# Smaller pieces on GpSimd and TensorE in the attention stage of a hybrid encoder block

## The chip, the cores and the metric

The kernel runs on one core of a Trainium2 chip. Its time is the time on the device in microseconds (us). One execution was taken by the hardware profiler; the others were only timed. TensorE does the matrix products, VectorE and ScalarE the elementwise work, GpSimd a few elementwise subtractions, and SyncE issues nearly all transfers (DMAs).

## The reference

One encoder block in float32 on 1024 tokens of 1024 channels, with 16 meta tokens in front:

```python
h = h + hybrid_mixer(rmsnorm(h, norm_mix), ...)      # pooling + gated linear attention, merged by gates
h = h + squared_relu_mlp(rmsnorm(h, norm_ffn), ...)  # relu(h w_ff1)^2 w_ff2
return rmsnorm(h, norm_final)[:, N_META:]

# in the mixer, z = u @ w_in is split into a, q, k, v, r, lr, ga, gb;
# the linear attention goes over chunks of 64 tokens, 4 heads (keys of 64, values of 128):
b = cumsum(a_c); decay = exp(-|b_t - b_s|)
o = (q k decay) v + (q exp(b)) S
S = exp(b_end) S + (k exp(b_end - b))^T v
m = sigmoid(ga) * y_a + sigmoid(gb) * y_b;  return m @ w_out
```

The meta tokens form a short first chunk; what the attention takes from them is the state S with which the first full chunk starts.

## The kernel before

**Split products.** Every float32 product is made of three products of rounded operands. An operand x is split into a high part (ScalarE copies it to a rounded type) and a low part (x minus the high part, by VectorE or GpSimd). `mm3` (L249 to L254) issues high x high, high x low and low x high for each of the 128-row slices, all added in one PSUM bank. Weights go through a ring of two slots: `Ring.top_up` (L76) loads a block of 1024 columns into a raw slot, splits it (L83 on ScalarE, L84 on `self.eng`) and has it ready one block ahead. `self.eng` is VectorE, but GpSimd from `gla_open` to the end of `gla`. Tiles of the raw, high and low parts are called raw, w1h and w1l.

**Stages.** From 0 to about 290 us come the norm, the gates, q, the pooling path and the first half of the values. From about 290 to 495 us runs the attention stage, `gla`; then the merge, where y_b is finished for the second half of the tokens and the product with w_out begins (about 495 to 560 us); then the feed-forward part to the end.

**The order in the attention stage.** TensorE's order is written out by hand, in the order in which the program issues. ScalarE, VectorE, GpSimd and SyncE are ordered by the framework's planner, from its own estimates of when things are ready; from `early_gates` on, the orders of ScalarE and VectorE are written out too. `gla` has two sorts of work:

- *Chains*, Python generators that issue one step and yield a number of us to be covered: `inside` (for a pair of heads and a half of the tokens: log decay, then scores and six levels of scores, L1187, each masked into the tile scc by VectorE, L1250, while VectorE and ScalarE grow the operands n and f of the next level, L1219 to L1221), `across` (transpose the keys, L1268; state updates, L1276 and then eight dependent VectorE steps, L1282; products with the values, L1289 and L1299; square, sum and norm, L1308 to L1313; transpose, L1317; multiply and split, L1318 to L1321), and `meta_state` (the meta tokens' state: a decay chain of small VectorE steps to L1157, a transposition on TensorE, L1160, its copy by VectorE, L1162, and, when the values are there, a small product, L1169).
- *Filler*: the key projections, the second value block `v_second` (9 tiles of 128 tokens, 24 products of 256 columns each, the last for the 16 meta tokens), the gates gb, and y_b for the first half of the tokens (`yb_block`; its low parts by GpSimd, L1105). Each filler chunk yields its estimated length: 0.64 us for three products of 512 columns, 2.56 us for a value tile.

In each round every live chain makes a step, and then `pour` issues filler for the largest wait asked for, times 1.1 (`PACE`), carrying what was poured too much to the next round:

```python
def pour(us):
    owed[0] += us
    while owed[0] > 0:
        cost = next(filler, None)
        if cost is None:
            return
        owed[0] -= cost
```

The chains of the second unit of the attention are `meta_state(1)`, `across` of the first unit and `inside` of the second, stepped in this order. Three PSUM banks (two of tag mm, one of tag mx) take turns for filler and meta steps.

**The merge.** `yb_block` for the second half multiplies by the gate (L1100), adds the pooling path (L1101) and splits (L1104, L1105); `load_wo` splits the blocks of w_out (L1402, L1403) that SyncE fetches (L1394). The fetch of the first blocks waits until the buffers of the attention stage, in whose place they land, have been read for the last time.

Of the kernel before, what the change touches and what calls it, by code (L numbers as in the profile page):

```python
# [8 lines left out]
F32 = mybir.dt.float32  # L9
# [3 lines left out]
ALU = mybir.AluOpType  # L13
# [6 lines left out]
KT = D // P  # L20
HALF = 512
# [37 lines left out]
class Ring:  # L59
# [16 lines left out]
    def top_up(self):  # L76
        while self.loaded < min(self.done + self.depth, len(self.queue)):
            s = self.loaded % self.depth
            if not self.fetched:
                self.fetch(1)  # L80
            raw, n = self.fetched.pop(0)
            hi, lo = self.hi[:, s, :n], self.lo[:, s, :n]
            self.nc.scalar.activation(hi, raw, ACT.Copy)  # L83
            self.eng.tensor_tensor(lo, raw, hi.bitcast(F32), ALU.subtract)  # L84
            self.views[self.loaded] = (hi, lo)
            self.loaded += 1

# [24 lines left out]
def kernel(  # L112
# [10 lines left out]
    act, dve, pool, pe = nc.scalar, nc.vector, nc.gpsimd, nc.tensor  # L123
# [20 lines left out]
    def bank(tag):  # L144
        if tag in rota:
            turn_of[tag] = turn_of.get(tag, -1) + 1
            tag = rota[tag][turn_of[tag] % len(rota[tag])]
        return psp[tag].tile([P, 512], F32, name=f"b_{tag}", tag=tag)
# [37 lines left out]
    raw = Raw(nc, [left.push(f"raw{i}", [P, D], F32) for i in range(2)])  # L186
# [10 lines left out]
    def f32(ap):  # L197
        return ap.bitcast(F32)
# [49 lines left out]
    def mm3(ps, n, lhs, rhs, first=True, last=True, more=False):  # L248

        for i in range(n):  # L250
            (ah, al), (bh, bl) = lhs(i), rhs(i)
            pe.matmul(ps, ah, bh, start=first and i == 0, stop=False, skip_group_check=more)  # L252
            pe.matmul(ps, ah, bl, start=False, stop=False, skip_group_check=more)  # L253
            pe.matmul(ps, al, bh, start=False, stop=last and i == n - 1, skip_group_check=more)  # L254
# [221 lines left out]

    vm = gB[32 : 32 + META, : 2 * 256]

    def v_tile(i, t, later=False, by_part=False):

        vw, w = S["vw"][i], 256 + 16 * (i == 0)
        if t == 8:
            half, at, n = 0, 0, META
        else:
            half, n = t // 4, P
            at = OFF[half] + (t % 4) * P
        b = bank("mm")[:n, :w]
        th, tl, hi, lo = TH[half][:, :, at : at + n], TL[half][:, :, at : at + n], vw[:, 0], vw[:, 1]
        parts = {"hh": (th, hi), "lh": (tl, hi), "hl": (th, lo)}
        left_of = {"n": 3}  # L490

        def part(name):
            left_of["n"] -= 1
            l, r = parts[name]
            for k in range(KT):
                pe.matmul(b, l[:, k], r[:, k], start=name == "hh" and k == 0, stop=left_of["n"] == 0 and k == KT - 1)

        if not by_part:
            mm3(b, KT, lambda k: (th[:, k], tl[:, k]), lambda k: (hi[:, k], lo[:, k]))

        def leave():
            if t == 8:
                act.activation(vm[:, i * 256 : i * 256 + 256], b[:, :256], ACT.Copy)
            else:
                act.activation(S["v"][i][:, t], b[:, :256], ACT.Copy)

        def leave_lr():
            if i == 0:
                act.activation(S["lrtok"][:n, t], b[:, 256:], ACT.Copy)

        if by_part:
            return part, (leave, leave_lr)
        if later:
            return leave, leave_lr
        leave()
        leave_lr()
# [87 lines left out]
    def start():  # L604
# [50 lines left out]
        with tc.manual_schedule(engines={mybir.EngineType.Activation, mybir.EngineType.DVE, mybir.EngineType.Pool}):  # L655
# [29 lines left out]
            hi(1)  # L685
            lr_lo = lr()
            v0, leave0 = v_tile(0, 0, by_part=True)
            v1, leave = v_tile(0, 1, by_part=True)
            v0("hh")
            for fn in lows[0]:  # L690
# [325 lines left out]

    def v_second():
        for t in range(9):
            v_tile(1, t)
            yield 24 * 256 / 2400  # L1020

    def yg_open():
        right.pop_to(0)
# [17 lines left out]
    def yb_load(n, h):  # L1041

        if n >= 8 or (n, h) in staged:
            return
        d = 2 * YB[h][n // 2] + n % 2
        gl, ml = staged[n, h] = (nxt("t2"), nxt("o2")) if h else (nxt("t1"), nxt("o"))
        nc.sync.dma_start(gl, gb_dram[d, h])
        nc.sync.dma_start(ml, ma_dram[d, h])
# [20 lines left out]
            yb_load(n, 1)  # L1069

    kept = {}

    def yb_block(n, h):
        j = YB[h][n]

        def fn(*wbs):
            if h == 0 and n > 1:
                kept[j] = wbs[0]
            wb = wbs[0] if wbs else kept[j]
            hi, lo = (t.rearrange("p (k c) -> p k c", k=4) for t in wb)  # L1080
            assert h or ("o", 0) in done
            yg = S["yg"][h]
            for e in range(2):
                d, w = 2 * j + e, slice(e * P, (e + 1) * P)
                for m in range(2 + h):
                    yb_load(2 * n + e + m, h)
                gl, ml = staged[2 * n + e, h]
                b = bank("mm")
                for k in range(4):
                    mm3(  # L1090
                        b, 1, lambda i: (hi[:, k, w], lo[:, k, w]),
                        lambda i: (yg[:, 0, k], yg[:, 1, k]), first=k == 0, last=k == 3,
                    )
                    yield 3 * 512 / 2400
                if e and not wbs:
                    W1.done, W1.kept = W1.done + 1, W1.kept - 1
                    W1.top_up()
                elif e:
                    yield "keep" if j in kept else "free"
                dve.tensor_tensor(gl, b, gl, ALU.mult)  # L1100
                dve.tensor_tensor(gl, gl, ml, ALU.add)  # L1101
                th = MH[h][:, d]
                tl = ML[h][:, d]
                act.activation(th, gl, ACT.Copy)  # L1104
                (dve if h else pool).tensor_tensor(tl, gl, f32(th), ALU.subtract)  # L1105

        return fn

# [5 lines left out]
    for p in range(2):  # L1114
        step(fill, k_block(p), W1, [w_cols(C_K + p * P)])
        told(("k", p))
    step(fill, v_second)
    step(fill, yg_open)
    told("v")
# [9 lines left out]
    def log_decay(lrT, p, n, dst, y, t, tag="ms"):  # L1129

        b, k = bank(tag)[:, :n], slice(0, 64 + RANK)
        pe.matmul(b, wgu[k, p * P : (p + 1) * P], lrT[k], start=True, stop=True)
        act.activation(y, b, ACT.Identity, bias=bgate[:, p : p + 1])
        act.activation(t, y, ACT.Abs)
        act.activation(t, t, ACT.Exp, scale=-1.0)
        act.activation(t, t, ACT.Ln, bias=1.0)
        dve.scalar_tensor_tensor(dst, y, 0.0, t, ALU.min, ALU.subtract)
# [4 lines left out]
    def twice(pre, suf, m):  # L1142

        pv, sv = blocks(pre, m), blocks(suf, m)
        nb = pre.shape[1] // (2 * m)
        end = lambda u: pv[:, :, u, m - 1 : m].broadcast_to([P, nb, m])
        dve.tensor_tensor(sv[:, :, 0], sv[:, :, 0], end(1), ALU.add)
        dve.tensor_tensor(pv[:, :, 1], pv[:, :, 1], end(0), ALU.add)

    def meta_state(p):  # L1150
        pre, suf, y, t = (metab[:, i] for i in range(4))
        log_decay(lrT_meta, p, META, pre, y, t, "mm")
        dve.memset(suf, 0.0)
        for m in (1, 2, 4, 8):
            twice(pre, suf, m)
        act.activation(y, suf, ACT.Exp, scale=1.0 / TAU)
        dve.tensor_tensor(y, y, S["kq"][0][:, p, 0, 0:META], ALU.mult)  # L1157
        yield 5.0
        b = bank("mm")
        pe.transpose(b[:META, :P], y, ident)  # L1160
        kt = gB[32 : 32 + META, 2 * 256 : 2 * 256 + P]
        dve.tensor_copy(kt, b[:META, :P])  # L1162
        yield 1.0
        while p and "v" not in done:
            yield 1.0
        b = bank("mm")
        for e in range(2):
            r = slice(e * CH, (e + 1) * CH)
            pe.matmul(  # L1169
                b[r, :P], kt[:, r], vm[:, (2 * p + e) * P : (2 * p + e + 1) * P], start=True, stop=True,  # L1170
                tile_position=(32, e * CH),
            )
        dve.tensor_copy(S["S"][:, 0, p], b[:, :P])
# [150 lines left out]
    def gla():  # L1324
# [12 lines left out]
        while ("k", 0) not in done:  # L1337
            next(filler)
        units = [(0, 0), (1, 0), (0, 1), (1, 1)]
        old, side = [], [meta_state(0)]  # L1340
        for n, u in enumerate(units + [None]):
            if u is None:
# [418 lines left out]
```

## Time and profile before

| | us |
|---|---|
| median of 3 runs | 1229.89 (1229.45 to 1230.79) |
| the profiled execution | 1232.42 |
| its span, first to last instruction | 1230.7 |
| TensorE busy | 1203.8 (98%) |
| VectorE busy | 856.4 (70%) |
| ScalarE busy | 618.4 (50%) |
| GpSimd busy | 54.1 (4%) |

PE is TensorE, PEld its weight loads, DVE VectorE, ACT ScalarE, POOL GpSimd, SP SyncE (SPq its queue). Rows of a timeline give the start in us from the span's start, the duration, the engine, the line, the operation and "written tile <- read tiles"; in brackets stands how long the engine was idle before and which instruction released it. In the table of waits an arrow points from the waiting instruction to the one waited for. Products overlap, so the spacing of their starts counts, not their durations.

### The profile page before, as it was taken

Reading aid. Unit: us, or ns where it says so; the run is one execution under the profiler, and the core shown is the slowest. Engines: PE = TensorE matmul, PEld = TensorE weight load, DVE = VectorE, ACT = ScalarE, POOL = GpSimd, SP = SyncE. Lnnn points to the kernel's source line nnn. Section 1 sums busy time; section 2 is a strip of 40 time slices with the busy share of each in tenths; the row PEclk is TensorE's granted clock in tenths of the full one; section 3 lists DMA queues with packets and bytes.
Section 4 is the critical chain, followed back from the end, with each engine's and each line's share of the span. In section 5 each row is a group of like instructions: output and inputs, shape, how many; then the busy total and the mean of one; then the engine's idle time right before and its main releaser. Section 6 shows DMA issues by size and latency. Waiting matters only on the chain.

```text
span 1230.7 us, 18292 instructions
## 1 busy us (share of the span) xinstructions
PE 1203.8 (98%) x6818; PEld 1002.2 (81%) x6818; DVE 856.4 (70%) x1399; ACT 618.4 (50%) x1099; POOL 54.1 (4%) x62
## 2 busy tenths in 40 slices
PE   7999999999999999999999999999999999999997
PEld 7878888978887877788878888888888888888885
DVE  7986675743566677734897676676775887887685
ACT  7677566322446753323655454554554444444544
POOL 2000000001101114000000000000000000000000
PEclk9999999999999999999999999999999999999999
DMA  8043326156102146651244444543569973333532
GB/s 252 2 113 121 117 86 189 52 171 189 36 19 72 59 154 215 209 201 52 104 134 157 145 154 148 167 155 129 177 216 329 335 251 99 99 94 95 171 95 86
DMA packets 141673, 173.85 MB, mean 141 GB/s; under 512 B 9944, under 2 KB 81392, under 8 KB 141584
## 3 DMA queue, kind: packets, MB, share of 16 engines
q1 hardware_dynamic: 141552, 172.62, 43.4%
q8 instruction: 54, 0.88, 0.3%
q14 instruction: 35, 0.29, 0.1%
q0 software_dynamic: 32, 0.07, 0.1%
HBM read 119.17 MB, written 53.48 MB: 140 GB/s over the span
## 4 chain that ended last, share of the span: by engine, by line
PE 84%; DVE 9%; ACT 3%; issue 2%; DMA 1%; POOL 0%; SPq 0%; DVEq 0%; ACTq 0%; POOLq 0%
PE b_mm L252 10%; PE b_mm L253 10%; PE b_mm L254 10%; PE b_ms L253 9%; PE b_ms L252 9%; PE b_ms L254 9%; PE b_x L253 8%; PE b_x L252 8%; PE b_x L254 8%; PE b_sc L1187 1%; PE b_mx L252 1%; PE b_m L1289 1%; DVE t L1101 1%; PE b_mx L254 1%; PE b_mx L253 1%
## 5 line engine op out<-in xcount | busy, mean ns | idle before, releaser
L252 PE MATMUL b_mm<-th,w1h 128*128 128x512 f32 (+1 forms) x312 | 118.3, 379 | 1.9 <-DVE c L800 1.0
L253 PE MATMUL b_mm<-tl,w1h 128*128 128x512 f32 (+1 forms) x312 | 116.7, 374 | 0.6 <-DVE tl L1464 0.6
L254 PE MATMUL b_mm<-th,w1l 128*128 128x512 f32 (+1 forms) x312 | 116.5, 373 | 0.0
L252 PE MATMUL b_x<-th,w1h 128*128 128x512 f32 (+1 forms) x240 | 90.8, 378 | 0.0
L253 PE MATMUL b_x<-tl,w1h 128*128 128x512 f32 (+1 forms) x240 | 90.7, 378 | 0.0
L254 PE MATMUL b_x<-th,w1l 128*128 128x512 f32 (+1 forms) x240 | 90.4, 377 | 0.0
L270 ACT ACTIVATE w1h<-raw 128x512 fp32r<-128x512 f32 x96 | 59.5, 621 | 32.8 <-PE b_ms L253 15.7
L271 DVE TENSOR_TENSOR w1l<-raw,w1h 128x512 fp32r<-128x512 f32 x96 | 65.7, 685 | 9.3 <-ACT w1h L270 9.3
L252 PEld LDWEIGHTS b_mm<-th,w1h 128*128 128x128 f32 x312 | 58.9, 189 | 13.5 <-issue 1.4
L270 ACT ACTIVATE w1h<-fs 128x512 fp32r<-128x512 f32 x72 | 45.3, 630 | 47.2 <-PE b_ms L253 32.2
L253 PEld LDWEIGHTS b_mm<-tl,w1h 128*128 128x128 f32 x312 | 59.1, 189 | 10.7 <-DVE tl L1464 0.9
L254 PEld LDWEIGHTS b_mm<-th,w1l 128*128 128x128 f32 x312 | 59.1, 189 | 10.5
L270 ACT ACTIVATE w1h<-bt 128x512 fp32r<-128x512 f32 x44 | 27.8, 632 | 67.1 <-issue 62.8
L271 DVE TENSOR_TENSOR w1l<-fs,w1h 128x512 fp32r<-128x512 f32 x72 | 49.3, 686 | 15.4 <-ACT w1h L270 15.3
L1618 DVE TENSOR_TENSOR bt<-w,w 128x512 f32<-128x512 f32 x80 | 54.8, 685 | 1.3 <-DMA w<-in_w_ff_dram 1.3
L254 PEld LDWEIGHTS b_x<-th,w1l 128*128 128x128 f32 x240 | 45.2, 188 | 8.5
L252 PEld LDWEIGHTS b_x<-th,w1h 128*128 128x128 f32 x240 | 45.1, 188 | 8.4
L253 PEld LDWEIGHTS b_x<-tl,w1h 128*128 128x128 f32 x240 | 45.1, 188 | 8.2
L270 ACT ACTIVATE fxh<-bt 128x512 fp32r<-128x512 f32 x36 | 22.8, 632 | 55.7 <-issue 50.1
L253 PE MATMUL b_ms<-wo,w1h 128*128 128x512 f32 x128 | 49.8, 389 | 0.0
L254 PE MATMUL b_ms<-wo,w1l 128*128 128x512 f32 x128 | 49.8, 389 | 0.0
L252 PE MATMUL b_ms<-wo,w1h 128*128 128x512 f32 x128 | 49.8, 389 | 0.0
(448 smaller groups left out, 3345.9 us busy)
## 6 DMA issues: line engine op xcount, KB each, us to landing
hf_dram<-h SPq DMA_DIRECT2D x112, 256.0 KB, 2.1
raw<-hf_dram SPq DMA_DIRECT2D x112, 256.0 KB, 2.7
w<-in_w_ff_dram SPq DMA_DIRECT2D x64, 256.0 KB, 4.5
raw<-in_w_in_dram SPq DMA_DIRECT2D x24, 512.0 KB, 4.7
raw<-in_w_ff_dram SPq DMA_DIRECT2D x16, 512.0 KB, 4.1
rawx<-in_w_ff_dram SPq DMA_DIRECT2D x16, 512.0 KB, 4.0
xs<-in_x_dram SPq DMA_DIRECT2D x8, 512.0 KB, 6.0
rawx<-in_w_in_dram SPq DMA_DIRECT2D x8, 512.0 KB, 4.4
```

The lines of the kernel that those rows point to most:

```text
L252: pe.matmul(ps, ah, bh, start=first and i == 0, stop=False, skip_group_check=more)
L253: pe.matmul(ps, ah, bl, start=False, stop=False, skip_group_check=more)
L254: pe.matmul(ps, al, bh, start=False, stop=last and i == n - 1, skip_group_check=more)
L270: act.activation(hi, a, ACT.Copy)
L271: dve.tensor_tensor(lo, a, f32(hi), ALU.subtract)
L1101: dve.tensor_tensor(gl, gl, ml, ALU.add)
L1187: pe.matmul(b[to, e, j], kk[r, s], qq[r, s], start=True, stop=True, tile_position=(e * CH, u * CH))
L1289: pe.matmul(o[part(u), e, j], scc[part(u), e, j], v[part(u), j, e], start=j == 0, stop=False, tile_position=(u * CH, u * CH), skip_group_c ...
L1618: dve.tensor_tensor(bt, w, S["w2"][q[3:]][:, i], ALU.add if q[2] == "+" else ALU.subtract)
```

## The change

Three edits. GpSimd's low parts are made in pieces of 256 columns: four in the ring, where GpSimd is its engine, and two in `yb_block` for the first half of the tokens; VectorE's stay whole. `v_second` issues each value tile as four quarters (two of the eight 128-row slices, six products), each yielding 0.64 us, and ScalarE's copy that empties the tile follows when the next chunk is asked for. `meta_state(1)` makes one empty step ahead of its transposition.

```diff
@@ Ring.top_up
-            self.eng.tensor_tensor(lo, raw, hi.bitcast(F32), ALU.subtract)
+            step = n if self.eng is self.nc.vector else n // 4
+            for at in range(0, n, step):
+                c = slice(at, at + step)
+                self.eng.tensor_tensor(lo[:, c], raw[:, c], hi[:, c].bitcast(F32), ALU.subtract)
@@ v_tile
-    def v_tile(i, t, later=False, by_part=False):
+    def v_tile(i, t, later=False, by_part=False, by_k=False):
...
-        if not by_part:
-            mm3(b, KT, lambda k: (th[:, k], tl[:, k]), lambda k: (hi[:, k], lo[:, k]))
+        def rows(k, n):
+            mm3(
+                b, n, lambda i: (th[:, k + i], tl[:, k + i]), lambda i: (hi[:, k + i], lo[:, k + i]),
+                first=k == 0, last=k + n == KT,
+            )
+
+        if not by_part and not by_k:
+            rows(0, KT)
...
+        if by_k:
+            return rows, leave
@@ v_second
         for t in range(9):
-            v_tile(1, t)
-            yield 24 * 256 / 2400
+            rows, leave = v_tile(1, t, by_k=True)
+            for k in range(0, KT, 2):
+                rows(k, 2)
+                yield 6 * 256 / 2400
+            leave()
@@ yb_block
+    halves_of_half = [slice(k * HALF // 2, (k + 1) * HALF // 2) for k in range(2)]
...
-                (dve if h else pool).tensor_tensor(tl, gl, f32(th), ALU.subtract)
+                if h:
+                    dve.tensor_tensor(tl, gl, f32(th), ALU.subtract)
+                for c in halves_of_half[: 2 - 2 * h]:
+                    pool.tensor_tensor(tl[:, c], gl[:, c], f32(th[:, c]), ALU.subtract)
@@ meta_state
         yield 5.0
+        if p:
+            yield 0.0
         b = bank("mm")
         pe.transpose(b[:META, :P], y, ident)
```

## The prediction

> **What bounds the kernel now.** I read the chain that ended last first, by engine, on the page; then a table of busy time by stretch; then the waits of TensorE.
>
> ```profile
> PE 84%; DVE 9%; ACT 3%; issue 2%; DMA 1%; POOL 0%; SPq 0%; DVEq 0%; ACTq 0%; POOLq 0%
> ```
>
> ```profile
> 0.00:290.00 290.00, 281.83 (x1458) 239.50 (x1459) 200.92 (x290) 169.47 (x307) 15.80 (x42) 1.00 0.42 128
> 290.00:520.00 230.00, 221.98 (x2255) 183.92 (x2254) 147.32 (x267) 112.24 (x191) 38.31 (x21) 1.00 0.34 108
> 520.00:1230.70 710.70, 699.95 (x3109) 578.77 (x3107) 508.12 (x844) 336.65 (x601) 0.00 (x0) 1.00 0.48 157
> ```
>
> The second number of a row is the stretch's length, then come the busy times of TensorE, its weight loads, VectorE, ScalarE and GpSimd, the granted clock and the DMA share. TensorE sets the time, at full clock. Everything that the diff touches runs between 290 and 520 us: there TensorE is idle for 230.00 - 221.98 = 8.0 us, and no edit removes work from it. So 8.0 us is the most that can be won, and the question is which of TensorE's waits the edits reach.
>
> ```profile
> PE b_m L1289 <- DVE S L1282: 1.6, 1, 1.6
> PE b_m L1317 <- DVE mix L1313: 1.5, 1, 1.5
> PE b_sc L1187 <- DVE scc L1250: 1.4, 2, 0.9
> PE b_mx L1160 <- DVE metab L1157: 0.8, 1, 0.8
> PE b_mm L253 <- DVE wo L1403: 0.8, 1, 0.8
> PE b_mm L252 <- ACT wo L1402: 0.5, 1, 0.5
> PE b_x L252 <- ACT w1h L83: 0.5, 1, 0.5
> PE b_x L254 <- DVE w1l L84: 0.5, 1, 0.5
> PE b_m L1289 <- DVE W L1282: 0.2, 1, 0.2
> ```
>
> These nine lines (total, times, longest, in us) make 7.8 of the 8.0 us. Most name VectorE. VectorE's and GpSimd's timelines show why it is late (start, duration, line, tiles):
>
> ```profile
> 325.96 2.53 DVE L1219 TENSOR_TENSOR n<-n,ends 128x512 f32<-128x512 f32 x1
> 394.83 2.76 DVE L1221 TENSOR_TENSOR f<-n,ends 128x512 f32<-128x512 f32 x1
> 398.27 0.35 DVE L1282 SCALAR_TENSOR_TENSOR S<-W,ends,b_m 128x128 f32<-128x128 f32 x1
> 402.51 0.68 DVE L1221 TENSOR_TENSOR f<-n,ends 128x512 f32<-128x512 f32 x1
> 428.08 2.92 DVE L1219 TENSOR_TENSOR n<-n,mix 128x512 f32<-128x512 f32 x1
> 466.07 2.26 DVE L1282 SCALAR_TENSOR_TENSOR W<-W,ends,b_m 128x128 f32<-128x128 f32 x6
> 475.20 2.90 DVE L1101 TENSOR_TENSOR t<-t,o 128x512 f32<-128x512 f32 x1
> 493.08 1.07 DVE L1101 TENSOR_TENSOR t<-t,o 128x512 f32<-128x512 f32 x1
> ```
>
> ```profile
> 325.55 2.39 POOL L84 TENSOR_TENSOR w1l<-raw,w1h 128x1024 fp32r<-128x1024 f32 x1 [11.48 <-ACT w1h L83]
> 394.64 2.41 POOL L84 TENSOR_TENSOR w1l<-raw,w1h 128x1024 fp32r<-128x1024 f32 x1 [11.32 <-ACT w1h L83]
> 427.62 2.81 POOL L84 TENSOR_TENSOR w1l<-raw,w1h 128x1024 fp32r<-128x1024 f32 x1 [13.56 <-ACT w1h L83]
> 463.57 1.29 POOL L1105 TENSOR_TENSOR tl<-t,th 128x512 fp32r<-128x512 f32 x1 [2.42 <-ACT th L1104]
> 465.57 2.40 POOL L84 TENSOR_TENSOR w1l<-raw,w1h 128x1024 fp32r<-128x1024 f32 x1 [0.71 <-ACT w1h L83]
> 474.64 2.90 POOL L84 TENSOR_TENSOR w1l<-raw,w1h 128x1024 fp32r<-128x1024 f32 x1 [1.29 <-ACT w1h L83]
> 491.86 3.45 POOL L1105 TENSOR_TENSOR tl<-t,th 128x512 fp32r<-128x512 f32 x2 [3.15 <-ACT th L1104]
> ```
>
> L1221 takes 0.68 us when GpSimd rests (402.51) and 2.76 us under a GpSimd subtraction: it ends at 397.59, one such duration after GpSimd's end at 397.05. The same at 325.96, 428.08 and 475.20. The six L1282 at 466.07, which read one operand from PSUM, run at 0.38 us each through GpSimd's 465.57 to 467.97 and wait for nothing. So a VectorE instruction with both inputs in SBUF stands still until the running GpSimd instruction ends, and the whole VectorE queue behind it. Taking 0.69 us off, the excess is 1.84 + 2.07 + 2.23 + 2.21 + 0.38 = 8.7 us, of which TensorE's waits took 0.94 + 1.6 + 0.2 + 1.5 = 4.2, about half.
>
> **The change, GpSimd's pieces.** GpSimd's two groups (count, busy us and mean ns, idle before):
>
> ```profile
> L84 POOL TENSOR_TENSOR w1l<-raw,w1h 128x1024 fp32r<-128x1024 f32 x10 | 24.9, 2490 | 129.6 <-ACT w1h L83 129.6
> L1105 POOL TENSOR_TENSOR tl<-t,th 128x512 fp32r<-128x512 f32 x8 | 12.0, 1511 | 14.9 <-ACT th L1104 14.9
> ```
>
> Undisturbed, a 1024-column subtraction costs 2.40 us, a 512-column one 1.29: 1.11 us for 512 columns, so 0.18 fixed and 0.555 per 256, 0.735 a piece. Four pieces are 2.94 us, 0.54 more than now; two halves of L1105 are 1.47, 0.18 more. There are 10 blocks and 8 tiles: 40 + 16 = 56 pieces. The added 5.4 + 1.4 us lies on GpSimd, which is busy 38.31 of 230 us. It delays w1l; the tightest case is the block of 474.64, ready at 477.54:
>
> ```profile
> 480.43 0.39 PE L254 MATMUL b_mm<-yg,w1l 128*128 128x512 f32 x1
> ```
>
> TensorE first reads it 2.9 us later, so 0.54 us, or twice that with a VectorE instruction taken between, is hidden; without that cover each block would cost what exceeds 2.9. SyncE's reload of the raw slot (L107), which waits for the last piece, moves as much; that slot is needed a block later.
>
> What VectorE gains: at 394.83 it now waits for the first piece only, to 394.64 + 0.735 = 395.37, and ends 0.69 later at 396.06 instead of 397.59: 1.53 us earlier. Behind it in the queue stand the L1282 that end in S at 398.62, for which TensorE's L1289 waits 1.6; as they ignore GpSimd, they come 1.53 earlier: **-1.5**. At 428.08 the wait on W is gone whenever the stall falls by over 0.2: **-0.2**. At 475.20, VectorE waits to 475.28 + 0.6 (the previous VectorE instruction ends at 475.28, the piece is already dispatched), ends near 476.6 instead of 478.10: 1.5 earlier. ScalarE's square, the norm and L1313 follow in a written order, so L1317 gets its operand 1.5 earlier and its wait of 1.5 shrinks to 0.1: **-1.4**.
>
> What is late next is the merge. There the last L1105 frees the buffers for a weight load:
>
> ```profile
> SPq L1394 <- POOL tl L1105: 5.1, 1, 5.1
> ```
>
> ```profile
> 500.10 1.06 ACT L1402 ACTIVATE wo<-acc 128x1024 fp32r<-128x1024 f32 x1 [1.08 <-DMA o<-ma_dram]
> ```
>
> SyncE issues it when GpSimd ends at 491.86 + 3.45 = 495.31; 4.8 us later ScalarE splits it, and behind that, in written order, stand the operands of TensorE's waits of 0.5, 0.5, 0.5 and 0.8. With four halves and VectorE in between, GpSimd ends between 0.2 later (two extra fixed parts of 0.18, less the stall that L1101 no longer passes on) and 2.3 later: four times (0.6 + 0.69) = 5.2 from 492.44, when L1101 before it ends, is 497.6. VectorE's own order is meanwhile up to 0.4 us earlier. I take **+0.5**, near the low end, because two of the four halves fall before the next VectorE instruction with two SBUF inputs is ready.
>
> **Quarter tiles.** The planner owes 1.6 x 1.1 = 1.76 us of filler after each score level, and pours while it owes more than nothing. A whole value tile counts 2.56, so after two tiles it owes -2.21, and 1.76 more leaves -0.45: level 4 follows level 3 without filler. With quarters of 0.64 the levels are 2, 3, 3, 3 and 2 quarters apart.
>
> ```profile
> 328.01 0.28 PE L254 MATMUL b_mm<-vw,tl 128*128 128x256 f32 x1
> 328.22 0.71 PE L1187 MATMUL b_sc<-n 64*64 64x64 f32 x32
> 328.86 0.39 PE L252 MATMUL b_mx<-vw,th 128*128 128x256 f32 x1
> 331.90 0.71 PE L1187 MATMUL b_sc<-n 64*64 64x64 f32 x32
> 333.56 0.71 PE L1187 MATMUL b_sc<-n 64*64 64x64 f32 x32 [0.94 <-DVE scc L1250]
> 366.18 0.71 PE L1187 MATMUL b_sc<-n 64*64 64x64 f32 x32 [0.43 <-DVE scc L1250]
> ```
>
> The pair at 331.90 and 333.56 is that place: level 4 waits 0.94 us for the copy of level 3. Three quarters, 18 matmuls at about 0.12 us, put 2.1 us between them: **-0.94**. A change from filler to scores and back costs 328.22 - 328.01 - 0.12 = 0.09 before and 0.39 - 0.28 = 0.11 after, 0.20 us. By the same account the steps that now stand back to back get filler between them at two places (levels 3 and 4; L1289 and L1299), two changes more: **+0.4**. The wait of 0.43 at 366.18 may go, since L1299 moves away from the level before it; the next two chunks are the same, so I take 0, with -0.43 as the other end. From L1169 on the account of both kernels is the same, so the order on TensorE is too. The ScalarE copy that empties a tile is now issued when the next is asked for; three banks take turns, so nothing waits.
>
> **The meta transposition.** L1160 waits 0.8 us. One round later it stands behind four transpositions, 32 scores and three quarters, some 3 us of TensorE; its VectorE copy moves with it, no DMA does, and the only reader, L1169, comes after the last value tile either way. The instruction that takes its place, L1268, transposes a tile that the previous unit finished: **-0.8**, between 0 (if VectorE, whose order the planner chooses, is as late for the scores) and -0.84.
>
> **The sum.** -1.5 - 0.2 - 1.4 + 0.5 - 0.94 + 0.4 - 0.8 = -3.94, say -4.0. The profiled execution took 1232.42 us with a span of 1230.70; the median of the runs shown, 1229.89, is 2.5 below it. So the span should be 1226.7, the execution 1228.4, the median **1225.9**.
>
> **The rivals.** First, *the merge takes it back*: GpSimd's last halves alternate with VectorE all the way and the w_out load starts 2.3 later rather than 0.5: 1225.9 + 1.8 = 1227.7. For it: 491.86 shows one alternation already (3.45 us for two of 1.29). Against: VectorE also has instructions without two SBUF inputs there.
>
> Second, *the pieces run as one*: GpSimd's queue closes the gap between them, so VectorE still waits for all four, now 0.54 longer: at 394.83, 428.08 and 475.20 TensorE loses 3 x 0.54 = 1.6 more, and the other edits bring -0.94 + 0.4 - 0.8: +0.3, 1230.2. Against it stands the pair at 491.86: the second was released at 493.1 while the first ran, and yet VectorE's L1101, issued at 493.08, ended at 494.15, before GpSimd's end at 495.31; it got in between. [...]
>
> Third, *slower*: VectorE pays a piece for each of several instructions, where it paid one long stall before. Five of GpSimd's 18 runs stalled VectorE in the rows above; if 30 of the 56 pieces did, at 0.6 us, that is 18 us of stall, half of it TensorE's: 9.0 against 4.2 now, +4.8 - 0.8 + 0.4 = +4.4 and 1234.3. It decides from about 24 pieces on (24 x 0.3 = 7.2, +3.0 - 0.4 = +2.6). At the present share 16 pieces would, most of them for part of a piece, in places where TensorE has 1 to 3 us of filler.
>
> That the change does nothing is excluded: the ring uses GpSimd throughout this stage, and other generators are live when the added empty step is taken.
>
> **How the numbers follow.** Forecast 0.55, the merge 0.20, one piece 0.09, slower 0.16. About 0.2%, 2.5 us, is what a measurement tells from no change, so faster is below 1227.4 and slower above 1232.4. Faster: 0.52 of the forecast and 0.04 of the merge, 0.56; slower: 0.14 of the third rival; same: 0.30. The forecast's own bounds are -0.43 and -0.5 (no loss in the merge), with some 1 us for the four late waits there, to 1223.5, and the merge at the top. The range runs to 1231.0, over the first two rivals, and leaves out 0.16 above and 0.03 below.
>
> **What would show it.** Right: no VectorE instruction of 512 columns above 1.4 us between 310 and 500; L1160 and the second score wait gone; L1289's and L1317's waits below 0.3; w_out split no later after the last L1105. Wrong: VectorE at 2.9 under four pieces (second rival); many at 1.2 to 1.4 with TensorE idle over 8 us (third); waits at L252 to L254 in the merge above 3.5 us in sum (first); another order on TensorE after L1169, or on VectorE before the gates, which the planner sets anew.

## The result, and the profile after

The changed kernel takes 1225.44 us (median of 5 runs, 1224.46 to 1225.56). The kernel before, run beside it, takes 1230.79 (5 runs, 1229.45 to 1233.54). The ratio is 0.9956, with an interval of 0.9946 to 0.9967: 5.3 us faster. The profiled execution took 1225.56 us with a span of 1222.7 us (before: 1232.42 and 1230.7).

Lines of the code have moved: the ring's low part L84 is now L87, GpSimd's low part of y_b is L1123 and VectorE's L1121 (both were L1105), the scores L1187 are L1207, L1289 is L1309, L1317 is L1337, and `mm3`'s three products L252 to L254 are L255 to L257.

The chain that ended last, by engine:

```profile
PE 87%; DVE 7%; ACT 2%; issue 2%; DMA 1%; POOL 0%; SPq 0%; DVEq 0%; ACTq 0%; POOLq 0%
```

The table of busy time by stretch, cut so that its first row ends at the same work as the middle row of before (the first product with w_out comes 5.13 us earlier, so 520 has become 515):

```profile
290.00:515.00 225.00, 221.94 (x2254) 183.76 (x2253) 145.15 (x267) 112.50 (x191) 47.04 (x59) 1.00 0.34 111
515.00:1222.70 707.70, 698.22 (x3108) 577.51 (x3107) 507.73 (x844) 336.84 (x601) 0.00 (x0) 1.00 0.48 158
```

TensorE's busy time in this stretch is what it was (221.94 against 221.98 us) and its idle time went from 8.0 to 225.00 - 221.94 = 3.1 us. That is a gain of 5.0 us, all of it waits. GpSimd is busy 8.7 us longer there (47.04 against 38.31) in 59 instructions instead of 21. TensorE's waits in this stretch:

```profile
PE b_mm L256 <- DVE wo L1423: 0.8, 1, 0.8
PE b_sc L1207 <- DVE scc L1270: 0.6, 1, 0.6
PE b_x L257 <- DVE w1l L87: 0.5, 1, 0.5
PE b_mm L255 <- ACT wo L1422: 0.5, 1, 0.5
PE b_mm L256 <- DVE yg L1341: 0.3, 1, 0.3
PE b_x L255 <- ACT w1h L83: 0.2, 1, 0.2
PE b_m L1309 <- DVE W L1302: 0.2, 1, 0.2
```

The two long waits for VectorE (1.6 at the state product, 1.5 at the merge of the gates) are gone, and so is that of the meta transposition (0.8). Of the two waits for the scores' copy, the one of 0.94 is gone; the other grew from 0.43 to 0.64. One small wait is new (0.3, for yg). VectorE's timeline shows how the long ones went, at the places shown of before:

```profile
393.02 1.09 DVE L1241 TENSOR_TENSOR f<-n,ends 128x512 f32<-128x512 f32 x1
...
394.79 0.35 DVE L1302 SCALAR_TENSOR_TENSOR S<-W,ends,b_m 128x128 f32<-128x128 f32 x1
...
424.60 1.21 DVE L1239 TENSOR_TENSOR n<-n,mix 128x512 f32<-128x512 f32 x1
425.74 0.96 DVE L1243 TENSOR_TENSOR ends<-mix 128x256 f32<-128x256 f32 x1
426.62 1.22 DVE L1241 TENSOR_TENSOR f<-n,mix 128x512 f32<-128x512 f32 x1
427.76 1.51 DVE L1243 TENSOR_TENSOR ends<-ends 128x128 f32<-128x128 f32 x4
```

And GpSimd's, where "x4" is a row of four pieces and the duration runs from the first's start to the last's end:

```profile
325.41 4.26 POOL L87 TENSOR_TENSOR w1l<-raw,w1h 128x256 fp32r<-128x256 f32 x4 [11.05 <-ACT w1h L83]
...
392.82 3.27 POOL L87 TENSOR_TENSOR w1l<-raw,w1h 128x256 fp32r<-128x256 f32 x4 [10.90 <-PE b_mm L257]
...
424.13 4.30 POOL L87 TENSOR_TENSOR w1l<-raw,w1h 128x256 fp32r<-128x256 f32 x4 [13.12 <-ACT w1h L83]
...
462.01 2.82 POOL L87 TENSOR_TENSOR w1l<-raw,w1h 128x256 fp32r<-128x256 f32 x4 [0.57 <-ACT w1h L83]
...
487.05 3.73 POOL L1123 TENSOR_TENSOR tl<-t,th 128x256 fp32r<-128x256 f32 x4 [3.15 <-ACT th L1119]
```

The instruction that stood 2.76 us under one whole subtraction (L1221 then) takes 1.09 us now: it starts at 393.02, ends at 394.11, and GpSimd is at work until 396.09. So VectorE gets in after the first piece and does not wait for the four. The state S follows at 394.79 and ends at 395.14, just before the product that reads it starts. The price can be seen as well: under 325.41 three VectorE instructions stall now (by 0.2, 0.5 and 0.5 us) and under 424.13 four (by 0.5 us each), where it was one before, and four pieces take 4.3 us there instead of the 2.82 at 462.01, where VectorE runs only instructions that read one operand from PSUM. Over the whole stage VectorE's stalls (each duration less the shortest of the same instruction) sum to some 6.5 us, against some 9 before. So the pieces do not do away with the stalls: they shorten the longest ones, for which TensorE waited.

The shift of TensorE's marks between the two traces shows where the time came from, step by step:

| TensorE's mark | before | after | gained in this stretch |
|---|---|---|---|
| first meta product (L1169, now L1189) | 321.26 | 321.12 | 0.14 (there from the start) |
| second meta product | 365.32 | 363.30 | 1.88: quarters and meta step |
| state product of the second unit (L1289, now L1309) | 398.76 | 395.28 | 1.46: pieces |
| the same, third unit | 437.58 | 434.01 | 0.09: pieces |
| merge of the gates, last (L1317, now L1337) | 483.70 | 478.61 | 1.52: pieces |
| first product with w_out | 511.80 | 506.67 | 0.04: the merge |
| end of the span | 1230.70 | 1222.70 | 2.87: some 1.7 not from the change, see the last section |

Up to the w_out product the gain is 5.1 us, close to the 5.3 of the medians. In the profiled execution of before, TensorE ran at half clock for 3.4 us in the feed-forward part, which none of the edits touches; this is 1.7 of the 2.9 us by which the two spans differ behind that product. The rest was not followed up; between other kernels whose clock held there, this last part differs by as much (717.61 us in `e1_pieces_only`, 716.07 in `e4_no_pieces`).

### The profile page after: what moved, and what is told of

Read it like the earlier page. It is cut to its first block, busy times and chain, and to the rows that moved or that the text cites. A ratio compares the mean times of both kernels' runs of the same rounds, so it can differ in the third digit from the quotient of the medians.

```text
span 1222.7 us, 18359 instructions
## 1 busy us (share of the span) xinstructions
PE 1202.0 (98%) x6818; PEld 1000.4 (82%) x6818; DVE 853.9 (70%) x1399; ACT 618.9 (51%) x1099; POOL 62.7 (5%) x100
## 4 chain that ended last, share of the span: by engine, by line
PE 87%; DVE 7%; ACT 2%; issue 2%; DMA 1%; POOL 0%; SPq 0%; DVEq 0%; ACTq 0%; POOLq 0%
PE b_mm L255 10%; PE b_mm L256 10%; PE b_mm L257 10%; PE b_ms L256 9%; PE b_ms L255 9%; PE b_ms L257 9%; PE b_x L256 8%; PE b_x L255 8%; PE b_x L257 8%; PE b_sc L1207 1%; PE b_mx L255 1%; PE b_mx L256 1%; PE b_mx L257 1%; PE b_m L1309 1%; DVE ut L776 1%
## 5 line engine op out<-in xcount | busy, mean ns | idle before, releaser
L255 PE MATMUL b_mm<-th,w1h 128*128 128x512 f32 (+1 forms) x312 | 117.6, 377 | 1.6 <-DVE c L811 1.0
L257 PE MATMUL b_mm<-th,w1l 128*128 128x512 f32 (+1 forms) x312 | 115.9, 371 | 0.0
L255 PE MATMUL b_x<-th,w1h 128*128 128x512 f32 (+1 forms) x240 | 90.8, 378 | 0.0
L257 PE MATMUL b_x<-th,w1l 128*128 128x512 f32 (+1 forms) x240 | 90.3, 376 | 0.0
L255 PEld LDWEIGHTS b_mm<-th,w1h 128*128 128x128 f32 x312 | 58.6, 188 | 13.2 <-issue 1.4
L257 PEld LDWEIGHTS b_mm<-th,w1l 128*128 128x128 f32 x312 | 58.6, 188 | 10.3
L257 PEld LDWEIGHTS b_x<-th,w1l 128*128 128x128 f32 x240 | 45.1, 188 | 8.5
L255 PEld LDWEIGHTS b_x<-th,w1h 128*128 128x128 f32 x240 | 45.1, 188 | 8.4
L255 PE MATMUL b_ms<-wo,w1h 128*128 128x512 f32 x128 | 49.8, 389 | 0.0
L257 PE MATMUL b_ms<-wo,w1l 128*128 128x512 f32 x128 | 49.8, 389 | 0.0
```

## The experiments

The theory was that the pieces end VectorE's stalls (about 3 us), and that the quarters and the meta step each take away a wait of their own. A first rival was that the order did it: where the planner orders an engine, other costs can give another order, and the pieces as such bring nothing. A second was that VectorE still waits for the whole run of pieces. All diffs are against the changed kernel; "before" is always the kernel before on the same chip.

**Each part alone, and two together.** Before: 1230.08 us.

`e1_pieces_only` takes the quarters and the meta step back:

```diff
-            rows, leave = v_tile(1, t, by_k=True)
-            for k in range(0, KT, 2):
-                rows(k, 2)
-                yield 6 * 256 / 2400
-            leave()
+            v_tile(1, t)
+            yield 24 * 256 / 2400
...
-        if p:
-            yield 0.0
```

> GpSimd's pieces alone; value tiles whole, transposition where it was. The orders of TensorE, VectorE and ScalarE are then those of the kernel before, instruction by instruction. Theory of the stall: VectorE waits for a piece instead of a block, so L1289's 1.63 us and L1317's 1.53 us go, the 0.23 shrinks, the waits of 0.94 and 0.84 stay: 3.0 to 3.5 us faster than before. Rival, the order: the gain comes from the new order on the engines that the other two edits bring, and pieces alone give under 1 us.

It took 1227.09 us, ratio 0.9972 (0.9962 to 0.9983): 3.0 us faster than before. TensorE's waits:

```profile
PE b_sc L1202 <- DVE scc L1265: 1.4, 2, 0.9
PE b_mx L1175 <- DVE metab L1172: 0.8, 1, 0.8
PE b_mm L256 <- DVE wo L1418: 0.8, 1, 0.8
PE b_x L257 <- DVE w1l L87: 0.5, 1, 0.5
PE b_mm L255 <- ACT wo L1417: 0.5, 1, 0.5
PE b_mm L256 <- DVE yg L1336: 0.3, 1, 0.3
PE b_m L1304 <- DVE W L1297: 0.2, 1, 0.2
```

Both long waits are gone, and the waits of the score levels (0.94 and 0.41) and of the meta transposition are as before. Apart from the cut itself, its trace has exactly the order of before on TensorE, VectorE, ScalarE and SyncE. So the gain of 3.0 us is not a matter of order.

`e2_quarters_only` has the quarters alone (low parts whole, no empty step); `e3_meta_only` has the empty step alone (low parts whole, value tiles whole); `e4_no_pieces` has both, with whole low parts:

```diff
-            step = n if self.eng is self.nc.vector else n // 4
-            for at in range(0, n, step):
-                c = slice(at, at + step)
-                self.eng.tensor_tensor(lo[:, c], raw[:, c], hi[:, c].bitcast(F32), ALU.subtract)
+            self.eng.tensor_tensor(lo, raw, hi.bitcast(F32), ALU.subtract)
...
-                if h:
-                    dve.tensor_tensor(tl, gl, f32(th), ALU.subtract)
-                for c in halves_of_half[: 2 - 2 * h]:
-                    pool.tensor_tensor(tl[:, c], gl[:, c], f32(th[:, c]), ALU.subtract)
+                (dve if h else pool).tensor_tensor(tl, gl, f32(th), ALU.subtract)
```

> Quarter tiles alone, GpSimd in whole blocks, transposition where it was. Theory of the stall: only the wait between score levels 3 and 4 goes, 0.94 us by the row and somewhat more by the spacing of the starts, against two changes between filler and chain at 0.2 each: 0.5 to 1.0 us faster; L1289's 1.6 and L1317's 1.5 stay. Rival, the order: 2 us or more, with the waits on VectorE under GpSimd's blocks shorter than 1 us.

> The transposition one step later alone. Theory of the stall: the 0.84 us wait at L1160 goes, everything else stays: 0.7 to 1.0 us faster. Rival, a wait that takes its place: VectorE is as late for the scores in the same round, and under 0.3 us is won.

> Quarter tiles and the later transposition, GpSimd in whole blocks: the changed kernel without its pieces, with the changed kernel's orders of TensorE, VectorE and ScalarE. Theory of the stall: 1.4 to 2.0 us faster than before, the changed kernel's 2.0 us at the meta product, with L1289's and L1317's waits of 1.6 and 1.5 still there, so 3.0 to 3.6 us slower than the changed kernel. Rival, the order: within 1 us of the changed kernel.

| kernel | us | ratio to before | TensorE, first scores to second meta product |
|---|---|---|---|
| before | 1230.08 | 1 | 47.65 |
| quarters alone | 1228.45 | 0.9988 (0.9979 to 0.9996) | 45.99 |
| meta step alone | 1228.96 | 0.9991 (0.9982 to 1.0) | 46.53 |
| both | 1228.57 | 0.9988 (0.9979 to 0.9997) | 45.86 |

The last column, from the traces, is sharper than the times: the quarters alone bring 1.66 us, the meta step alone 1.12, both together 1.79. They do not add. The quarters alone brought more than the 0.5 to 1.0 us that was expected of them, the meta step about what was expected. The waits of the quarters alone say why:

```profile
PE b_m L1301 <- DVE S L1294: 1.6, 1, 1.6
PE b_m L1329 <- DVE mix L1325: 1.5, 1, 1.5
PE b_mm L253 <- DVE wo L1415: 0.8, 1, 0.8
PE b_sc L1199 <- DVE scc L1262: 0.6, 1, 0.6
```

There is no wait at the meta transposition, though it was not moved. With whole tiles the planner's account poured two tiles (5.12 us) between the last decay step and the round in which the transposition stands; with quarters it pours nine (5.76 us), and VectorE is done by then. The 0.8 us was taken away by the quarters already, and the meta step, which would have taken it alone, found nothing left but 0.1 us. The two long waits stay in all three kernels; in that with both parts:

```profile
PE b_m L1303 <- DVE S L1296: 1.6, 1, 1.6
PE b_m L1331 <- DVE mix L1327: 1.5, 1, 1.5
```

This kernel has the changed kernel's order on TensorE, VectorE, ScalarE and SyncE and still has the stalls. With `e1_pieces_only` this refutes the rival of the order from both sides.

**The size of a piece, and no GpSimd.** Before: 1230.81 us. The ring's blocks in two pieces of 512 columns (`e5_ring_512`, below) and in eight of 128 (`e6_ring_128`, the same with `n // 8`); and all these low parts by VectorE (`e8_no_gpsimd`):

```diff
-            step = n if self.eng is self.nc.vector else n // 4
+            step = n if self.eng is self.nc.vector else n // 2
```

```diff
-        W1.eng = pool
+        W1.eng = dve
...
-                if h:
-                    dve.tensor_tensor(tl, gl, f32(th), ALU.subtract)
-                for c in halves_of_half[: 2 - 2 * h]:
-                    pool.tensor_tensor(tl[:, c], gl[:, c], f32(th[:, c]), ALU.subtract)
+                dve.tensor_tensor(tl, gl, f32(th), ALU.subtract)
```

> The changed kernel with ring pieces of 512 columns instead of 256; all engines' orders as in the changed kernel. Theory of the stall (VectorE waits for the running piece alone): a piece is 1.29 us rather than 0.7, so the update of f and n under it ends about 0.5 us later, L1289 and L1317 wait some 0.4 to 0.6 us each: 0.8 to 1.3 us slower than the changed kernel, 3.9 to 4.5 faster than the one before. Rival, the pieces run as one: no difference.

> Ring pieces of 128 columns. By the rows of the changed kernel a piece of 256 takes 0.705 us undisturbed and a whole block 2.40, so each cut costs 0.14 us and a piece of 128 takes 0.44: eight are 3.4 us. Theory of the stall: no wait of TensorE in the changed kernel's attention stage is left to a ring piece but 0.15 us, so within 0.3 us of the changed kernel. Rival, more pieces catch more VectorE instructions: VectorE's excess grows and 1 us or more is lost.

> The changed kernel, but VectorE makes the low parts that GpSimd made (10 of 1.23 us and 8 of 0.69, 17.8 us more on VectorE in a stretch where it is busy 143 of 222 us). Theory: the work is worth more than the stalls it brings in pieces (about 4 us of excess left), TensorE waits for VectorE at the state updates and in the last unit: 2 to 6 us slower than the changed kernel. [...]

With 512 columns the kernel takes 1226.82 us, ratio 0.9966 (0.9953 to 0.9978), 1.4 us more than the changed kernel's median. The two intervals overlap; the traces are sharper: from the first scores to the first w_out product it is 190.33 us, against 189.12 and 189.50 in two traces of the changed kernel. VectorE's and GpSimd's timelines at the second unit:

```profile
393.39 1.66 DVE L1241 TENSOR_TENSOR f<-n,ends 128x512 f32<-128x512 f32 x1
```

```profile
393.21 2.98 POOL L87 TENSOR_TENSOR w1l<-raw,w1h 128x512 fp32r<-128x512 f32 x2 [11.18 <-PE b_mm L257]
```

VectorE comes 0.18 us after the first piece has begun and takes 1.66 us: the rest of that piece (1.29 - 0.18 = 1.1) and some 0.6 of its own. For both pieces it would have needed 2.4 + 0.6. So it waits for the piece that runs and for no more; the rival of pieces that run as one is refuted here, at a second size. TensorE's wait for S comes back as 0.5 us, and that for the gates as 0.5:

```profile
PE b_m L1309 <- DVE S L1302: 0.5, 1, 0.5
PE b_mm L255 <- ACT wo L1422: 0.5, 1, 0.5
PE b_m L1337 <- DVE mix L1333: 0.5, 1, 0.5
```

With 128 columns it takes 1225.88 us, ratio 0.9958 (0.9945 to 0.9972): no better than 256 columns, and 0.4 us worse by the medians, which is within the noise (189.36 us from the first scores to the first w_out product). With whole blocks the wait for S is 1.6 us, with pieces of 512 columns 0.5, with 256 and 128 none. Once TensorE's wait is used up, a smaller piece buys nothing.

Without GpSimd it takes 1233.81 us, ratio 1.0026 (1.0017 to 1.0035): 8.4 us slower than the changed kernel and 3.0 slower than before. The waits that grew or are new:

```profile
PE b_x L255 <- ACT w1h L83: 1.8, 1, 1.8
PE b_mm L255 <- ACT yg L1337: 1.8, 1, 1.8
PE b_m L1316 <- DVE small L1311: 1.5, 1, 1.5
```

Two of the three name ScalarE, but ScalarE itself waits for VectorE there: 1.89 us for the tile mix ahead of yg, and 2.62 us for the tile t in the copy just ahead of w1h. The low parts are added to VectorE ahead of what TensorE waits for. So GpSimd is worth keeping in this order of work, and the stalls are the smaller evil. The 2 to 6 us that were expected left out the clock: in the profiled execution it fell twice on top, for some 1.7 us each (last section).

**The merge.** `e9_merge_pool` lets GpSimd make the first six low parts of y_b's second half too, in halves; `e7_tiles_whole` keeps the ring's pieces but cuts no low part of y_b; in another series `e9_again` and `e11_changed_again` repeat the former and the changed kernel on one chip with `e7_tiles_whole`.

```diff
-                if h:
+                if h and n == 3:
                     dve.tensor_tensor(tl, gl, f32(th), ALU.subtract)
-                for c in halves_of_half[: 2 - 2 * h]:
-                    pool.tensor_tensor(tl[:, c], gl[:, c], f32(th[:, c]), ALU.subtract)
+                else:
+                    for c in halves_of_half:
+                        pool.tensor_tensor(tl[:, c], gl[:, c], f32(th[:, c]), ALU.subtract)
```

> The changed kernel, with GpSimd making in halves also the low parts of the first six tiles of the second half of the tokens, which VectorE makes one after another in the merge. Theory: VectorE's written order there (gate, sum, wait of 0.7 for ScalarE, low part of 0.69) is what TensorE's last waits in the merge hang on (0.2, 0.5, 0.5 and 0.8 us); 1.4 us less a tile takes most of the 2.0 us away: 1.0 to 2.0 us faster than the changed kernel. Rival, the wait moves: GpSimd's halves are late for the loads that take over their buffers, or stall VectorE's next instruction, and nothing is won or up to 2 us lost.

> The changed kernel with the low parts of the first half's tiles in one GpSimd instruction each, ring pieces kept. If GpSimd's last halves cost what the prediction put down for the merge (0.5 us), this is 0.5 us faster than the changed kernel; if VectorE's shorter stalls pay for GpSimd's later end, as the changed profile suggests, it is within 0.2 us, with VectorE's L1341 no longer stalled but its sum and low part by 0.3 to 0.4 us instead.

> The version with the merge's first six low parts on GpSimd once more, beside the changed kernel: by its trace 0.5 us faster than the changed kernel (the waits in the merge came down from 2.0 to 1.4 us); if that was chance, within 0.2 us.

> The changed kernel once more, beside the two others of this call, so that they are compared on one chip: 0.9950 to 0.9965 of the kernel before.

| kernel | us | ratio to before |
|---|---|---|
| `e9_merge_pool` (before: 1230.81) | 1224.65 (1224.06 to 1225.21) | 0.9949 (0.9937 to 0.9961) |
| `e9_again` (before: 1230.44) | 1224.90 (1224.47 to 1225.48) | 0.9953 (0.9941 to 0.9965) |
| `e7_tiles_whole` (before: 1230.44) | 1224.82 (1224.05 to 1225.20) | 0.9951 (0.9938 to 0.9965) |
| `e11_changed_again` (before: 1230.44) | 1225.19 (1225.03 to 1225.50) | 0.9956 (0.9943 to 0.9968) |

Whole low parts of y_b are 0.4 us quicker than halves on the same chip, and its waits in this stage are those of the changed kernel without the one for yg, and with 0.5 instead of 0.2 for w1h.

The difference is within the noise, so all that can be said is that the cut of y_b's low parts brings nothing that can be measured; the ring's pieces bring the gain of the first edit. More of the merge on GpSimd brought 0.3 to 0.8 us where I expected more: the waits change places. Its waits of the merge (0.9 for w1l, 0.5 for wo) sum to 1.4 us where the changed kernel has 0.2 + 0.5 + 0.5 + 0.8 = 2.0. None of these versions is clearly quicker than the changed kernel.

## Why the prediction was right, and where its steps were wrong

The forecast was 1225.9 us; 1225.44 was measured, from a gain of 5.3 us where the sum had 4.0 (the forecast started from 1229.89, the three runs shown, and the five runs beside the changed kernel have 1230.79). That the two times lie within 0.5 us is in part luck: the gain was forecast 1.3 us too small, and the start was 0.9 us too low.

- **The pieces: right, in size too.** Forecast -1.5, -0.2 and -1.4; the marks show -1.46, -0.09 and -1.52, and the part alone 3.0 us. The step behind it, that a waiting VectorE instruction gets in between two queued GpSimd instructions, was read from one pair of rows (L1101 at 493.08); the 512-column pieces and the rows at 393.02 now show it. The wait on W went from 0.23 to 0.15 only: its L1239 did shorten from 2.92 to 1.21 us, but three instructions behind it (425.74, 426.62 and one of the four at 427.76) now stall by 0.5 us each, so W came only a little earlier. One instruction, f<-n,ends, took 2.76 us under a whole block (394.83 of before), 1.66 under a piece of 512 columns (393.39 of `e5_ring_512`) and 1.09 under one of 256 (393.02), against 0.68 with GpSimd at rest. The second rival, that the pieces run as one, holds only where no VectorE instruction waits: there queued pieces follow one another without a gap (462.01, four in 2.82 us, starting 0.70 us apart). With waiting VectorE instructions in between four took 4.26 and 4.30 us (325.41 and 424.13).
- **The 0.94 was not a stall's.** The prediction counted the wait of 0.94 us at the fourth level among those that GpSimd's stalls cost TensorE (4.2 of 8.7 us). VectorE had been idle ahead of the copy that level 4 waited for:

```profile
332.68 0.73 DVE L1250 COPY_PREDICATED scc<-mask,b_sc 128x512 f32<-128x512 uint8 x1 [1.75 <-PE b_sc L1187]
```

  The pieces alone left the 0.94 as it was. So the stalls cost TensorE 3.3 us, not 4.2, and the share of "about half" in the third rival was too high. The sum isn't touched, as it gave the 0.94 to the quarters.
- **A piece's price: 0.735 forecast, 0.705 measured** (2.82 for four). The ring's group shows the mean, with VectorE in between, of 0.841:

```profile
L87 POOL TENSOR_TENSOR w1l<-raw,w1h 128x256 fp32r<-128x256 f32 x40 | 32.3, 841 | 124.7 <-ACT w1h L83 73.6 <-PE b_mm L257 51.2
```

- **Quarters and meta step: the sum nearly right, its parts wrong.** Forecast -0.94 + 0.4 for the quarters and -0.8 for the step, -1.34 together; measured -1.79 to -1.88 together, of which the quarters alone take -1.66. The step that failed is that the account of the planner was followed for the score levels only. The same account, carried on to the transposition, would have given nine quarters instead of two tiles ahead of it, and the 0.8 would have stood with the quarters. The +0.4 for two more changes between filler and scores can't be seen: the waits alone changed by -0.94 - 0.84 + 0.21 = -1.57, and the marks by more than that. A part of this is that the idle time in a row is counted from the modelled end of the product before, so that it is some 0.1 us short of what the marks show: the scores at 331.90 and 333.56 start 1.66 us apart where 0.64 would do (328.22 to 328.86), 1.02 us, while the row has 0.94.
- **The wait of 0.43 at the third level: taken as unchanged, bounds 0 to -0.43; it became 0.64.** The bounds left out that it could grow. It grew with the quarters (0.64 in `e2_quarters_only` and `e4_no_pieces`, 0.40 and 0.41 in the kernels without them), so it belongs to what TensorE now has, or has not, between the levels of the second unit. What would take it away wasn't tried.
- **The merge: +0.5 forecast, some 0.3 found.** GpSimd's last low part does come later by 0.56 us, seen from the gates' product (478.61 to 490.78, before 483.70 to 495.31), as forecast. Between these two profiles nothing came of it, because w_out is split 4.2 us after that instead of 4.8:

```profile
494.96 1.06 ACT L1422 ACTIVATE wo<-acc 128x1024 fp32r<-128x1024 f32 x1 [0.50 <-DMA t<-gb_dram]
```

  From the gates' product to the first w_out product it is 28.06 us after and 28.10 before. But before is the longest of the five kernels with whole low parts of y_b: the others have 27.61, 27.72, 27.72 (`e2_quarters_only`, `e3_meta_only`, `e4_no_pieces`) and 28.04 (`e7_tiles_whole`). With halves it is 28.06, 27.95, 28.09, 28.23 and 28.37 (the changed kernel, `e1_pieces_only`, `e5_ring_512`, `e6_ring_128` and the repeat). The means are 27.84 and 28.14. The time from GpSimd's end to the split, 4.1 to 4.8 us, differs by more than that from one execution to the next, so one pair of profiles can't show the price. The first rival, which had this cost at 2.3, is refuted.
- **The rival on the other side**, many short stalls in place of one long one, is real as a mechanism (three instructions under 325.41, four under 424.13, by 0.2 to 0.5 us each), but hardly a TensorE wait stands behind it. Of the ring's ten blocks only these two took 4.3 us; six took 2.8, with no VectorE instruction held up by 0.1 us or more, and two 3.3 and 3.5.
- **The sum came out 1 us short of the gain**, mostly in the quarters and meta step (0.5) and in the merge's 0.5, of which these two profiles show nothing.

Of what would have shown the steps wrong, one thing came in part: VectorE's and ScalarE's orders changed, by a few instructions around the value tiles and the meta copy ahead of L1169, and behind that nothing changed on any engine. What was named for "right" came: no VectorE instruction of 512 columns exceeds 1.23 us between 310 and 500. One of 1024 columns, yg (483.46), takes 1.52 us, 0.3 more than without a stall. The wait of 0.31 for yg is all that this stall left on TensorE.

## What to carry to other kernels

In this kernel a GpSimd subtraction on SBUF held up VectorE's instructions with two SBUF inputs, and all that stood behind them in the queue, to its end: 2.76 us instead of 0.68 under a block of 2.41. Cut such work into pieces as short as TensorE's slack needs: here 256 columns; 128 brought nothing more (1225.88 us against 1225.44), while each cut cost GpSimd some 0.14 us (2.82 us in four pieces, 2.40 in one) and the last piece comes later. Cut what stands beside a chain that TensorE waits for; cutting the rest, y_b's low parts, brought nothing. Where two edits aim at two waits in one chain, follow the account of poured work to the second wait with the first edit in place, for the first may take both.

## What the runs showed of the hardware that was not expected

**TensorE's clock fell to half for 3.4 us after a short stretch with waits.** Rows of the table of busy time in the feed-forward part of before; the last number but two is the granted clock, 0.50 in the second row:

```profile
619.70:623.11 3.41, 1.89 (x7) 1.24 (x7) 3.41 (x7) 2.42 (x5) 0.00 (x0) 1.00 0.00 0
623.11:626.53 3.42, 3.42 (x9) 2.65 (x8) 2.93 (x5) 1.52 (x3) 0.00 (x0) 0.50 0.00 0
```

The products there follow each other at 0.43 us instead of 0.23:

```profile
622.69 0.39 PE L253 MATMUL b_mm<-tl,w1h 128*128 128x512 f32 x1
622.91 0.45 PE L254 MATMUL b_mm<-th,w1l 128*128 128x512 f32 x1
623.16 0.63 PE L252 MATMUL b_mm<-th,w1h 128*128 128x512 f32 x1
623.59 0.63 PE L253 MATMUL b_mm<-tl,w1h 128*128 128x512 f32 x1
```

At half speed 3.41 us do the work of 1.7, so 1.7 us are lost. Ahead of it stand two waits of 0.89 and 0.64 us (ending at 620.75 and 621.88). The profile of `e3_meta_only` lost its clock in the same place, after waits of 1.01 and 0.63 us, and `e8_no_gpsimd` twice, at 490.95 after waits of 1.8 and 0.8 us in the merge and at 511.43 after 1.8 and 0.5 us. `e9_again` kept it at the place of before, after waits of 0.86 and 0.63 us: the products behind them stay 0.23 us apart.

Where more than one change of the clock can be read in a trace, they lie a whole number of 3.413 us apart. Before, the clock falls at 623.11 and again at 1227.27, behind TensorE's last product: 604.16 us, 177 times 3.413. In `e8_no_gpsimd` the two falls are 20.48 us apart, six times 3.413. Before, both waits fell into one such stretch, in which TensorE was busy 1.89 of 3.41 us (first row above). In the changed kernel's profile the clock falls at 1219.85, behind the last product; counted back from there in steps of 3.413 us, waits of 0.61 and 0.64 us fell into two stretches, and the clock held:

```profile
612.28:615.70 3.42, 2.81 (x12) 1.80 (x10) 3.42 (x7) 2.54 (x5) 0.00 (x0) 1.00 0.01 4
615.70:619.11 3.41, 2.77 (x13) 2.22 (x13) 3.41 (x7) 1.93 (x5) 0.00 (x0) 1.00 0.00 0
```

That it matters how the waits fall into such stretches is a reading of these few places; no run tests it by itself. Around these two waits, the least that TensorE was busy in any 3.41 us was 1.77 us in `e3_meta_only` and 1.89 before, where the clock was lost, and 1.93 in `e9_again` and 1.99 in `e1_pieces_only`, where it held. Busy time doesn't tell it everywhere, though: in the attention stage `e4_no_pieces` was busy 1.78 of 3.41 us (393.94 to 397.35, with a wait of 1.64 us) and kept its clock, with products 0.23 us apart from 399.77 on. What decides it stays open.

Such falls also go with a part of the spread of the kernel before. In 8 of the 54 runs of before with a clock on record its mean was 0.997, and these took 1231.99 us in the mean, while the other 46, at 0.998 or 0.999, took 1230.25: a difference of 1.7 us, as much as one such fall costs. None of the ten runs of the changed kernel was below 0.998. Since most runs of before have no such loss, the gain of 5 us is not from it.

**Each cut of GpSimd's subtraction cost 0.14 us.** Undisturbed, 1024 columns take 2.40 us in one piece (465.57 of before) and 2.82 in four (462.01 of the changed kernel), and 512 columns 1.29 in one (463.57 of before) and 1.43 in two (460.01 of the changed kernel).

**A VectorE instruction with one SBUF input was stalled too.** Under two halves on GpSimd, a small instruction with a scalar took 0.55 us, where the same operation took 0.17 a little later:

```profile
475.79 0.55 DVE L220 TENSOR_SCALAR small<-small 128x8 f32<-128x8 f32 x1
...
476.85 0.17 DVE L227 TENSOR_SCALAR small<-small 128x8 f32<-128x8 f32 x1
```

```profile
474.88 1.43 POOL L1123 TENSOR_TENSOR tl<-t,th 128x256 fp32r<-128x256 f32 x2
```

It ends at 476.34, just after GpSimd at 476.31. In `e7_tiles_whole` it took 0.41 us and ended at 476.73, after GpSimd at 476.70; without GpSimd's work (`e8_no_gpsimd`) it took 0.17. So the count of SBUF inputs alone doesn't tell which VectorE instruction stalls.
